# The first MLP product by Strassen's scheme on 576-token groups, its hidden rows passed through DRAM, in a hybrid diffusion layer on Trainium2

## The chip, the cores and the metric

The kernel runs on one core of one Trainium2 chip, in one launch. The metric is the device time of one execution in microseconds (us). TensorE multiplies matrices into PSUM (eight banks of 512 float32 columns per partition), VectorE, ScalarE and GpSimd do the elementwise work, and SyncE (SP) issues most of the DMAs. An engine carries out its instructions in the order in which they are written; engines wait for one another by semaphores.

## The reference, cut to what matters

One layer acts on 128 prompt tokens and 1024 sample tokens of width 1024. A mixer of retention and a diagonal state-space scan comes first, then its output projection with a residual and a row norm, then the MLP. The change concerns the MLP alone:

```python
h = _norm(x) * (1.0 + sc2) + sh2                       # (1152, 1024)
f = jnp.square(jax.nn.relu(h @ w_ff1 + b_ff1)) @ w_ff2 + b_ff2
x = _ln_affine(ALPHA * x + g2 * f, ln2_g, ln2_b)       # w_ff1 (1024, 4096), w_ff2 (4096, 1024)
```

The modulation `sc2, sh2, g2` of the prompt tokens differs from that of the sample tokens. Everything is float32.

## The kernel before, in words

A float32 operand x is split into a rounded part hi and a rest lo = x - hi, both of type float32r (`split`, L195: a copy on ScalarE or VectorE, a subtraction on VectorE or GpSimd). A product of two split operands is three matmuls, hi x hi, hi x lo and lo x hi, into one PSUM bank (`mm3`, L208 to L210). Most tiles of SBUF are 30 slots of 128 x 1152 words (`slot`, `rel`): a freed slot goes to the end of a list, and a new tile takes the head of it, so a tile waits for whoever used its slot before. The order of the instructions on each engine is the order in which this file writes them.

The 1152 tokens are nine row tiles ("slots" 0 to 8 in the code, `sl`) of 128. The output projection `op_mm` (L1472 to L1474) takes a row tile at a time, 48 matmuls of 512 columns; `op_a` and `op_b` make the residual, the row norm and its gain; `op_c` writes the row tile to DRAM (RD) and, for the row tiles 0 to 2, norms it again for the MLP. Between the projections of row tiles 5 and 6 `make_h2` transposes the normed row tiles, modulates them on ScalarE and splits them.

The MLP runs in three groups g of 384 tokens. Each group has 32 steps f, one for each 128 hidden units. In a step `ff1` makes 24 matmuls of 384 columns (8 blocks of the inner dimension, three each), ScalarE adds the bias, takes Relu and Square, and `split` makes the hidden rows for the second product. `ff2` adds this step's share to the six accumulators of the group: three row tiles, two halves, three matmuls of 512 columns each, 18 in all (L1620 to L1622). The loop writes `ff1` of step i+1 ahead of `ff2` of step i:

```python
        f_load(i + 3)
        f_split(i + 2, 0)
        f_split(i + 1, 1)
        ...
        if i + 1 < 3 * NF:
            ff1(i + 1)
        if g < 2 or f < NF - TAIL:
            ff2(i)
```

`f_load` has SP load a block of both weight matrices, 0.5 MB each (L1535, L1536); so each weight is loaded and split three times, once a group. `h2_prep` and `make_h2` make the next group's operand in steps 14 to 27 of a group. At a group's end `ep1` takes the accumulators out of PSUM times the gate (L1660), and `ep2` and `ep3` make the residual (L1665), the last row norm (L157 to L182), gain (L1668) and bias (L1669) and store the rows, in steps 1, 3 and 5 of the next group. In the last group the second product of the last six steps (TAIL) is kept to the end and done a row tile at a time, and `last_rows` ends the last tile.

Of the kernel before, what the change touches and what calls it, by code (L numbers as in the profile page):

```python
# [9 lines left out]
F32 = mybir.dt.float32  # L10
# [21 lines left out]
def kernel(  # L32
# [36 lines left out]
    free, held = list(range(NS)), {}  # L69

    def slot(name, dt=F32):

        i = free.pop(0)
        t = slots.tile([P, SLOTF], dt, tag=f"b{i}", name=nm(name), bufs=1)
        held[t.name] = i
        return t
# [1418 lines left out]
    def op_c(sl, x, *_):  # L1495
        a = x[:, 0:D]
        gl(RD[sl], a)
        if sl < 3:
# [6 lines left out]
    h2T = {}  # L1505

    def make_h2(g, k0=0, k1=KT):
        if k0 == 0:
            h2T[g] = group_slots("h2")
        at = h2T[g]  # L1510
        for kt in range(k0, k1):
            pt = ps("h2t")
            for i in range(3):
                PE.transpose(pt[:, i * P:(i + 1) * P], h2n[3 * g + i][:, kt * P:(kt + 1) * P], ident)
            h = t384("h")
            for a, b, cd in (((0, 128, 1), (128, 384, 0)) if g == 0 else ((0, 384, 0),)):
                S.activation(h[:, a:b], pt[:, a:b], AF.Identity, bias=modT[:, 24 + kt, cd:cd + 1], scale=modT[:, 32 + kt, cd:cd + 1])
            split(at(kt, 0), at(kt, 1), h, "v", "p")
        if k1 == KT:
            for i in range(3):  # L1520
                rel(h2n.pop(3 * g + i))
# [5 lines left out]
    fw = {}  # L1527

    def f_load(i):

        if i >= 3 * NF or i in fw:
            return
        f = i % NF
        r1, r2 = slot("w1r"), slot("w2r")
        ld(r1[:, 0:D].rearrange("p (k n) -> p k n", k=KT), w_ff1[0].rearrange("(k p) n -> p k n", p=P)[:, :, f * P:(f + 1) * P])  # L1535
        ld(r2[:, 0:D], w_ff2[0, f * P:(f + 1) * P, :])  # L1536
        fw[i] = [r1, r2]

    def f_split(i, which, leng="v"):
        if i >= 3 * NF:  # L1540
            return
        hi, lo = slot("wh", F32R), slot("wl", F32R)
        split(hi[:, 0:D], lo[:, 0:D], fw[i][which][:, 0:D], "s", leng)
        rel(fw[i][which])
        fw[i][which] = (hi, lo)

    pend = {}
    for sl in range(9):
# [15 lines left out]
        if sl == 5:  # L1564
            f_load(0)
        if sl == 6:
            f_split(0, 0, "v")
            f_split(0, 1, "p")
            f_load(1)
    for kt in range(4, 8):  # L1570
        rel(*wo[kt])
    f_load(2)
    if stop <= 6:
        for sl in range(9):
            t = slot("dbg")
            ld(t[:, 0:D], RD[sl])
            dump(f"x1_{sl}", t[:, 0:D])
        return


    fp = []

    def fvec(src):
        t = fp[0].tile([P, D], F32, tag="fvec", name=nm("fvec"), bufs=5)
        ld(t, src.partition_broadcast(P))
        return t

    hid, x1t = {}, {}

    def ff1(i):  # L1590
        g, f = divmod(i, NF)
        pu = ps("ff1")
        wh, wl = fw[i][0]
        for kt in range(KT):
            k = slice(kt * P, (kt + 1) * P)
            mm3(pu[:, 0:384], wh[:, k], wl[:, k], h2T[g](kt, 0), h2T[g](kt, 1), kt == 0, kt == KT - 1)
        r = t384("r")
        S.activation(r, pu[:, 0:384], AF.Relu, bias=bf1[:, f:f + 1])  # L1598
        S.activation(r, r, AF.Square)
        hh = slot("hid", F32R)[:, 0:768].rearrange("p (a n) -> p a n", a=2)  # L1600
# [3 lines left out]
        if f == NF - 1:  # L1604
            rel(*h2T[g].tiles.values())
# [186 lines left out]
```

## Time and profile before

| | |
|---|---|
| median of 3 runs (lowest to highest) | 1431.72 us (1427.59 to 1432.12) |
| the profiled execution, its time | 1430.16 us |
| its span in the trace | 1428.4 us |
| granted TensorE clock over the span, mean | 0.982 of 2.4 GHz |
| HBM read, written | 186.31 MB, 27.02 MB |

The page gives for each engine the time in which at least one of its instructions ran. TensorE's matmuls are pipelined: one lasts longer than the distance from its start to the next one's start, and it is that distance, called the pitch below, that adds up. A stage's table shows busy times in a stretch of the span; a timeline row shows the start and the duration of one instruction, or of several merged. Idle time in square brackets stands ahead of an instruction, with what ended it.

### The profile page before, as it was taken

The page shows a single profiled execution, that of the slowest core. Times are in us where ns is not written, and L with a number is a line of the kernel's source. Part 1 is how long each engine was busy: PE and PEld are TensorE (multiplying, and loading weights), DVE is VectorE, ACT ScalarE, POOL GpSimd, SP SyncE. Part 2 cuts the span into 40 slices and gives each one's busy share as a digit, 9 for nine tenths or more (in the row PEclk, how much of TensorE's full clock was granted, in tenths as well). Part 3 has the DMA queues.
Part 4 walks back from the last instruction along what each step waited for, and adds up shares of the span by engine and source line. Part 5 has one row for each costly group of instructions (what it writes and reads, how often), then busy time and mean ns, then how long its engine had stood idle before and what let it go on. Part 6 is the DMA issues. An engine that isn't in the chain of part 4 may idle for free.

```text
span 1428.4 us, 19630 instructions
## 1 busy us (share of the span) xinstructions
PE 1356.3 (95%) x7631; PEld 1223.9 (86%) x7631; DVE 817.9 (57%) x1477; ACT 593.7 (42%) x993; POOL 236.9 (17%) x298
## 2 busy tenths in 40 slices
PE   5899999996998899989999999999999999999996
PEld 2799799986987788879999999989999998999995
DVE  6597979693266767773444334654543367433346
ACT  4467112121435532344445543444544444444351
POOL 2600000563535212530000100100001001000002
PEclk9999999998999999999999999999999999999998
DMA  9435631756995151376353333474433424743321
GB/s 317 130 98 154 227 105 31 211 161 209 258 312 141 53 192 58 117 255 219 118 166 115 118 118 118 146 231 139 148 116 110 135 94 138 245 136 118 122 85 45
DMA packets 186813, 214.62 MB, mean 150 GB/s; under 512 B 20056, under 2 KB 150624, under 8 KB 186208
## 3 DMA queue, kind: packets, MB, share of 16 engines
q1 hardware_dynamic: 167968, 174.65, 38.5%
q0 software_dynamic: 9648, 31.52, 7.3%
q10 hardware_dynamic: 9104, 7.19, 1.6%
q8 instruction: 60, 0.98, 0.3%
q14 instruction: 33, 0.27, 0.1%
HBM read 186.31 MB, written 27.02 MB: 149 GB/s over the span
## 4 chain that ended last, share of the span: by engine, by line
PE 66%; DVE 14%; ACT 5%; issue 5%; DMA 4%; POOL 3%; SPq 0%; ACTq 0%; POOLq 0%; DVEq 0%
PE ff L210 8%; PE ff L208 8%; PE ff L209 8%; PE acc L1622 8%; PE acc L1621 8%; PE acc L1620 7%; PE pu L209 3%; PE pu L208 3%; PE pu L210 3%; DMA w1r<-in_w_ff_dram 2%; DMA SD<-SB 1%; PE pv L692 1%; DVE st L157 1%; DVE st L158 1%; DVE wl L201 1%
## 5 line engine op out<-in xcount | busy, mean ns | idle before, releaser
L201 DVE TENSOR_TENSOR hid<-r,hid 128x384 fp32r<-128x384 f32 x96 | 67.5, 703 | 339.6 <-ACT hid L200 339.4
L208 PE MATMUL ff<-h,wh 128*128 128x384 f32 x768 | 258.8, 337 | 0.0
L210 PE MATMUL ff<-h,wl 128*128 128x384 f32 x768 | 257.8, 336 | 0.1
L209 PE MATMUL ff<-h,wh 128*128 128x384 f32 x768 | 257.3, 335 | 0.0
L1622 PE MATMUL acc<-wh,hid 128*128 128x512 f32 x564 | 222.8, 395 | 5.0 <-DVE hid L201 5.0
L1620 PE MATMUL acc<-wh,hid 128*128 128x512 f32 x564 | 220.5, 391 | 4.3 <-ACT hid L200 4.3
L1621 PE MATMUL acc<-wl,hid 128*128 128x512 f32 x564 | 221.8, 393 | 0.0
L1598 ACT ACTIVATE r<-ff,bf 128x384 f32<-128x384 f32 x96 | 55.6, 579 | 304.8 <-PE ff L210 304.8
L208 PE MATMUL pu<-hTh,wh 128*128 128x384 f32 x480 | 165.6, 345 | 0.7 <-ACT hTh L571 0.7
L209 PE MATMUL pu<-hTl,wh 128*128 128x384 f32 x480 | 162.7, 339 | 1.5 <-DVE hTl L574 1.4
L210 PE MATMUL pu<-hTh,wl 128*128 128x384 f32 x480 | 161.7, 337 | 1.1 <-POOL wl L201 1.1
L201 DVE TENSOR_TENSOR wl<-w1r,wh 128x1024 fp32r<-128x1024 f32 x96 | 117.5, 1224 | 61.8 <-ACT wh L200 57.2
L208 PEld LDWEIGHTS ff<-h,wh 128*128 128x128 f32 x768 | 144.2, 188 | 2.9
L209 PEld LDWEIGHTS ff<-h,wh 128*128 128x128 f32 x768 | 144.2, 188 | 2.9
L210 PEld LDWEIGHTS ff<-h,wl 128*128 128x128 f32 x768 | 144.1, 188 | 0.5 <-DVE wl L201 0.5
L1622 PEld LDWEIGHTS acc<-wh,hid 128*128 128x128 f32 x564 | 106.4, 189 | 29.3 <-DVE hid L201 7.0
L1620 PEld LDWEIGHTS acc<-wh,hid 128*128 128x128 f32 x564 | 106.5, 189 | 24.8 <-ACT hid L200 4.9
L1621 PEld LDWEIGHTS acc<-wl,hid 128*128 128x128 f32 x564 | 106.4, 189 | 20.6
L201 DVE TENSOR_TENSOR wl<-w2r,wh 128x1024 fp32r<-128x1024 f32 x95 | 120.2, 1265 | 0.9 <-PE acc L1622 0.6
L200 ACT ACTIVATE wh<-w1r 128x1024 fp32r<-128x1024 f32 x96 | 100.5, 1047 | 28.4 <-DMA w1r<-in_w_ff_dram 27.9
L200 ACT ACTIVATE wh<-w2r 128x1024 fp32r<-128x1024 f32 x96 | 100.3, 1045 | 0.0
L208 PEld LDWEIGHTS pu<-hTh,wh 128*128 128x128 f32 x480 | 91.0, 190 | 6.7 <-issue 4.1
(480 smaller groups left out, 2089.4 us busy)
## 6 DMA issues: line engine op xcount, KB each, us to landing
w1r<-in_w_ff_dram SPq DMA_DIRECT2D x96, 512.0 KB, 4.5
w2r<-in_w_ff_dram SPq DMA_DIRECT2D x96, 512.0 KB, 5.1
wa<-in_w_ada_dram SPq DMA_DIRECT2D x48, 512.0 KB, 8.0
wr<-in_w_in_dram SPq DMA_DIRECT2D x20, 512.0 KB, 4.0
SD<-SB POOLq DMA_DIRECT2D x8, 576.0 KB, 12.5
WD<-W POOLq DMA_DIRECT2D x8, 576.0 KB, 4.1
RD<-xr POOLq DMA_DIRECT2D x9, 512.0 KB, 3.1
x<-RD SPq DMA_DIRECT2D x9, 512.0 KB, 7.6
```

The costliest lines, as they stand in the source:

```text
L157: V.bn_stats(st[:, 0], x[:, 0:512])
L158: V.bn_stats(st[:, 1], x[:, 512:1024])
L200: S.activation(hi, x, AF.Copy)
L201: (tt if leng == "v" else PO.tensor_tensor)(lo, x, hi.bitcast(F32), SUB)
L208: PE.matmul(out, lhsT=wh, rhs=xh, start=first, stop=False)
L209: PE.matmul(out, lhsT=wh, rhs=xl, start=False, stop=False)
L210: PE.matmul(out, lhsT=wl, rhs=xh, start=False, stop=last)
L692: PE.matmul(pv[64 * g2:64 * g2 + 64, l * NCOL:(l + 1) * NCOL], lhsT=W[:, g * P + ri * 64:g * P + ri * 64 + 64], rhs=X[:, g], start=True, s ...
L1598: S.activation(r, pu[:, 0:384], AF.Relu, bias=bf1[:, f:f + 1])
L1620: PE.matmul(o, lhsT=hh[:, 0, tk], rhs=wh[:, cs], start=(f == 0), stop=False)
L1621: PE.matmul(o, lhsT=hh[:, 0, tk], rhs=wl[:, cs], start=False, stop=False)
L1622: PE.matmul(o, lhsT=hh[:, 1, tk], rhs=wh[:, cs], start=False, stop=(f == NF - 1))
```

## The change

The first product is done for two groups of 576 tokens instead of three of 384. A group's operand h (1024 x 576) is cut into four blocks of 512 x 288, and a pair of weight blocks (1024 x 256) into four of 512 x 128. Strassen's scheme (in Winograd's form) makes the four result blocks of 128 x 288 from seven products of sums of blocks, each 4 x 3 = 12 matmuls of 288 columns. The sums of h are made once a group (`h2_sums`, two on VectorE and two on GpSimd, then `h2_split`). Those of the weights are made in each step (`f_prep`: two sums on VectorE, two on GpSimd, seven splits), one step ahead. The products are added up as they leave PSUM, by one copy on ScalarE and seven additions on VectorE.

The two products no longer take turns. The steps are: 16 of the first product for tokens 0 to 575, 32 of the second for tokens 0 to 383, 16 of the first for tokens 576 to 1151, then 32 and 32 of the second for the other two groups of 384 tokens. The hidden rows after the Square are written to a DRAM tensor HD by SP and loaded again, as float32, in the second product's steps, where they are split. The prompt and the next four row tiles are normed in the projection's loop now (`op_c`, five instead of three); twelve further slots replace the pool `fp`; the gates, gains and biases of the epilogue are loaded when they are needed and freed again; the first group's epilogue is moved into the second group's first product, with its additions and its gain on GpSimd.

```diff
+    HT = 288
+    def make_h2(g, kt):
+        if kt == 0:
+            BLK.update({(j, l): slot("hb") for j in range(2) for l in range(2)})
+        pa, pb = ps("h2t"), ps("h2t")
+        for i in range(4):
+            PE.transpose(pa[:, i * P:(i + 1) * P], h2n[i + 5 * g][:, kt * P:(kt + 1) * P], ident)
+        PE.transpose(pb[:, 0:P], h2n[4][:, kt * P:(kt + 1) * P], ident)
...
+        for o, x, cd in parts:
+            S.activation(o, x, AF.Identity, bias=modT[:, 24 + kt, cd:cd + 1], scale=modT[:, 32 + kt, cd:cd + 1])
...
+    def h2_sums(n):
+        b11, b12, b21, b22 = (BLK.get(k) for k in ((0, 0), (0, 1), (1, 0), (1, 1)))
+        if n == 0:
+            BLK["t1"] = slot("hb")
+            tt(BLK["t1"], b12, b11, SUB)
+        elif n == 1:
+            BLK["t2"] = slot("hb")
+            tt(BLK["t2"], b22, BLK["t1"], SUB)
+        elif n == 2:
+            PO.tensor_tensor(b12, b22, b12, SUB)
+        else:
+            BLK["t4"] = slot("hb")
+            PO.tensor_tensor(BLK["t4"], b21, BLK["t2"], SUB)
...
+    HD = drp.tile([NF, P, NTOK], F32, name="HD")
+    STEPS = [(1, 0, p) for p in range(16)] + [(2, 0, f) for f in range(NF)] + [(1, 1, p) for p in range(16)]
+    STEPS += [(2, g, f) for g in (1, 2) for f in range(NF)]
...
+    def f_prep(i):
+        if STEPS[i][0] == 2:
...
+            split(hi[:, 0:D], lo[:, 0:D], r[:, 0:D], "s")
...
+            split(hid[i][:, 0:384], hid[i][:, 384:768], h[:, 0:384], "s")
...
+        tt(s1, a21, a22, ADD)
+        tt(s2, s1, a11, SUB)
+        PO.tensor_tensor(s3, a11, a21, SUB)
+        PO.tensor_tensor(s4, a12, s2, SUB)
+        yield
+        for n, x in enumerate((a11, s2, s1, s3, a12, a22, s4)):
+            t = ops[n] = slot("wop", F32R)
+            split(t[:, 0:512], t[:, 512:D], x, "s")
...
+            yield
...
     for sl in range(9):
...
         if sl == 7:
-            f_split(1, 0, "v")
+            op_mm(7, 0, 4)
+            for kt in range(5, 8):
+                make_h2(0, kt)
+        x, po = op_mm(sl, 3 if sl < 3 else 4 if sl == 7 else 0)
+        if sl == 6:
+            for kt in range(5):
+                make_h2(0, kt)
+            f_load(0)
+        if sl == 7:
+            for n in range(4):
+                h2_sums(n)
+            h2_split(0)
...
+    op_c(7, *pend.pop(7))
+    prep(0, 2)
+    h2_split(1)
+    prep(0, 1)
...
+    h2_split(3, "p")
...
     def ff1(i):
...
+        for n in range(7):
+            o = bank[n] = ps("ff1")[:, 0:HT]
+            w, (xh, xl) = ops[n], hop[n]
+            for q in range(4):
+                wh, wl = w[:, q * P:(q + 1) * P], w[:, 512 + q * P:512 + (q + 1) * P]
+                xs = slice(q * HT, (q + 1) * HT)
+                mm3(o, wh, wl, xh[:, xs], xl[:, xs], q == 0, q == 3)
+            rel(w)
+            if n == 0:
+                S.copy(p1, o)
+            elif n == 1:
+                tt(u2, o, p1, ADD)
...
+            yield
...
+            S.activation(cv, cv, AF.Square)
+            ld(HD[2 * p + q][:, g * 576:(g + 1) * 576], cv)
...
+    for i, (kind, g, f) in enumerate(STEPS):
+        prep(i)
+        for j in range(i + 1, min(i + 4, NST)):
+            if STEPS[j][0] == 2 or j <= i + 2:
+                f_load(j)
+        if kind == 1:
...
+            if g == 1 and f in (2, 4, 6):
+                ep_add(f // 2 - 1, PO)
+            if g == 1 and f in (3, 5, 7):
+                ep2(f // 2 - 1, True)
...
+            prep(i + 1, 1)
+            for _ in ff1(i):
+                prep(i + 1, 1)
+            continue
+        if STEPS[i + 1][0] == 2 if i + 1 < NST else False:
+            prep(i + 1)
...
+        if g == 0:
+            if 1 <= f < 6:
+                h2_prep(9 - f)
+            if 8 <= f < 16:
+                make_h2(1, f - 8)
...
+        if g == 2 and f in (1, 3, 5):
+            sl = 3 + f // 2
+            ep_add(sl)
             ep2(sl)
             ep3(sl)
```

## Rows read from the trace of the kernel before

**Rows 1.** The page, part 1: engine, busy us (share of span), instructions.

```profile
PE 1356.3 (95%) x7631; PEld 1223.9 (86%) x7631; DVE 817.9 (57%) x1477; ACT 593.7 (42%) x993; POOL 236.9 (17%) x298
```

**Rows 2.** The page, part 4: the chain that ended last, by engine.

```profile
PE 66%; DVE 14%; ACT 5%; issue 5%; DMA 4%; POOL 3%; SPq 0%; ACTq 0%; POOLq 0%; DVEq 0%
```

**Rows 3.** Table of stages: stretch, us, busy by engine, granted clock, DMA, GB/s.

```profile
core 0: us, PE busy (x) PEld busy (x) DVE busy (x) ACT busy (x) POOL busy (x), PEclk, DMA share, GB/s
...
609.00:621.50 12.50, 7.10 (x21) 5.16 (x20) 10.10 (x21) 4.60 (x7) 2.90 (x2) 0.73 0.84 275
622.00:700.00 78.00, 77.86 (x396) 71.18 (x397) 38.05 (x35) 36.05 (x51) 9.49 (x4) 1.00 0.61 202
...
880.00:940.00 60.00, 57.54 (x290) 51.73 (x289) 42.34 (x59) 28.24 (x41) 7.16 (x3) 1.00 0.28 89
1150.00:1250.00 100.00, 98.63 (x497) 89.09 (x496) 61.21 (x77) 46.48 (x66) 7.19 (x3) 1.00 0.47 152
1250.00:1350.00 100.00, 100.00 (x508) 91.08 (x507) 36.18 (x37) 42.40 (x60) 0.00 (x0) 1.00 0.39 128
```

**Rows 4.** Timeline of TensorE, one MLP step: start us, duration us, instruction.

```profile
700.82 0.39 PE L1620 MATMUL acc<-wh,hid 128*128 128x512 f32 x1
...
704.94 0.33 PE L208 MATMUL ff<-h,wh 128*128 128x384 f32 x1
...
709.13 0.39 PE L1620 MATMUL acc<-wh,hid 128*128 128x512 f32 x1
```

**Rows 5.** Timeline of TensorE, matmuls and transposes of 128 columns (xN merged).

```profile
376.89 0.60 PE L1219 MATMUL pk<-ident,qkv 128*128 128x128 f32 x4
377.32 0.60 PE L1221 MATMUL pv<-ident,qkv 128*128 128x128 f32 x4
...
390.76 0.38 PE L1235 MATMUL pkf<-qkv,qkv 128*128 128x128 f32 x2
...
393.21 0.39 PE L1235 MATMUL pkb<-qkv,kb 128*128 128x128 f32 x2
```

**Rows 6.** Timeline of TensorE, start of the MLP.

```profile
608.91 0.34 PE L210 MATMUL ff<-h,wl 128*128 128x384 f32 x1
612.85 0.50 PE L1620 MATMUL acc<-wh,hid 128*128 128x512 f32 x1 [3.60 <-ACT hid L200]
...
621.49 0.34 PE L208 MATMUL ff<-h,wh 128*128 128x384 f32 x1
```

**Rows 7.** Timeline of VectorE, the last group's epilogue.

```profile
1401.50 1.23 DVE L1665 TENSOR_TENSOR o<-o,x 128x1024 f32<-128x1024 f32 x1
...
1407.17 1.22 DVE L1668 TENSOR_TENSOR o<-o,fvec 128x1024 f32<-128x1024 f32 x1 [1.37 <-ACT o L1667]
...
1409.66 2.35 DVE L1665 TENSOR_TENSOR o<-o,x 128x1024 f32<-128x1024 f32 x1
...
1417.83 1.57 DVE L1692 TENSOR_TENSOR o<-o,x 128x512 f32<-128x512 f32 x1
```

**Rows 8.** Timeline of GpSimd, the last group's epilogue.

```profile
1408.53 2.39 POOL L1669 TENSOR_TENSOR o<-o,fvec 128x1024 f32<-128x1024 f32 x1 [199.05 <-issue]
1416.49 2.35 POOL L1668 TENSOR_TENSOR o<-o,fvec 128x1024 f32<-128x1024 f32 x1 [5.57 <-ACT o L1667]
```

**Rows 9.** Timeline of VectorE, the subtractions of one MLP step.

```profile
702.75 0.56 DVE L201 TENSOR_TENSOR hid<-r,hid 128x384 fp32r<-128x384 f32 x1 [3.86 <-ACT hid L200]
...
703.70 1.23 DVE L201 TENSOR_TENSOR wl<-w1r,wh 128x1024 fp32r<-128x1024 f32 x1 [0.39 <-ACT wh L200]
704.84 1.22 DVE L201 TENSOR_TENSOR wl<-w2r,wh 128x1024 fp32r<-128x1024 f32 x1
```

**Rows 10.** The page, part 5: ScalarE's copy of a split: count, busy us, mean ns.

```profile
L200 ACT ACTIVATE wh<-w1r 128x1024 fp32r<-128x1024 f32 x96 | 100.5, 1047 | 28.4 <-DMA w1r<-in_w_ff_dram 27.9
```

**Rows 11.** The page, part 6: loads, KB each, median us from issue to landing.

```profile
w1r<-in_w_ff_dram SPq DMA_DIRECT2D x96, 512.0 KB, 4.5
```

More of the change, by code (lines that the diff above doesn't have):

```diff
@@ L67, in ps @@
         return psp.tile([P, 512], F32, tag="ps", name=nm(name))
-    free, held = list(range(NS)), {}
+    NX = 12
+    free, held, xpool = list(range(NS)), {}, []
     def slot(name, dt=F32):
         i = free.pop(0)
-        t = slots.tile([P, SLOTF], dt, tag=f"b{i}", name=nm(name), bufs=1)
+        t = (slots if i < NS else xpool[0]).tile([P, SLOTF], dt, tag=f"b{i}", name=nm(name), bufs=1)
         held[t.name] = i
@@ L1503, in op_c @@
             rel(x)
[L1505 to L1521, printed above, removed]
+    HT = 288
@@ L1524, with h2_split @@
+    def h2_split(n, leng="v"):
+        x = BLK.pop(HKEYS[n])
+        hop[n] = slot("hop", F32R), slot("hop", F32R)
+        split(*hop[n], x, "s", leng)
+        rel(x)
     NF = 32
@@ L1539, in f_split @@
-    def f_split(i, which, leng="v"):
-        if i >= 3 * NF:
-            return
[L1542 to L1545, printed above, removed]
+        kind, g, f = STEPS[i]
+        fw[i] = []
+        if kind == 1:
+            for q in range(2):
+                r = slot("w1r")
+                c0 = (2 * f + q) * P
+                ld(r[:, 0:D].rearrange("p (k n) -> p k n", k=KT), w_ff1[0].rearrange("(k p) n -> p k n", p=P)[:, :, c0:c0 + P])
+                fw[i].append(r)
+        else:
+            r = slot("w2r")
+            ld(r[:, 0:D], w_ff2[0, f * P:(f + 1) * P, :])
+            hid[i] = slot("hid")
+            ld(hid[i][:, 0:384], HD[f][:, g * 384:(g + 1) * 384])
+            fw[i].append(r)
@@ L1547, with prep @@
+    def prep(i, n=99):
+        if i >= NST:
+            return
+        if i not in preps:
+            f_load(i)
+            preps[i] = f_prep(i)
+        for _ in range(n):
+            if next(preps[i], 0) == 0:
+                break
     pend = {}
@@ L1563 @@
         op_b(sl, *pend[sl])
[L1564 to L1569, printed above, removed]
+    op_c(7, *pend.pop(7))
+    prep(0, 2)
+    h2_split(1)
+    prep(0, 1)
     for kt in range(4, 8):
         rel(*wo[kt])
[L1572 to L1581, printed above, removed]
+    h2_split(2)
@@ L1630, in x1_load @@
             sl = 3 * g + i
-            x1t[sl] = fp[0].tile([P, D], F32, tag="x1", name=nm("x1"), bufs=3)
-            ld(x1t[sl], RD[sl])
+            x1t[sl] = slot("x1")
+            ld(x1t[sl][:, 0:D], RD[sl])
     def h2_prep(sl):
@@ L1656, in ep1 @@
         gv = vecs["g2p" if sl == 0 else "g2s"]
-        o = fp[0].tile([P, D], F32, tag="o", name=nm("o"), bufs=3)
+        o = slot("o")
         for hf in range(2):
```

231 lines of the change are left out of this document (151 added, 80 removed).

## The prediction

> **What bounds the kernel now.** I read the page's busy shares first, then the chain that ended last, then a table of stages, then single steps of TensorE. The reader is to see TensorE busy for 1356 of 1428 us while VectorE stands at 57% and GpSimd at 17% [rows 1], and two thirds of the last chain on TensorE [rows 2]. In the table TensorE is never idle from 1250 to 1350 and for 77.86 of 78 us from 622 to 700, at the full granted clock (1.00, that is 2.4 GHz) [rows 3]. So in the MLP, from 600.7 us to the end, time is TensorE's instruction count times its pitch, plus a few stalls. One step there is 18 matmuls of the second product (700.82 to 704.94, 4.12 us, 0.2289 us each) and 24 of the first (704.94 to 709.13, 4.19 us, 0.1746 us each) [rows 4]. The stalls are at the start (last matmul of the opening at 608.91, next at 612.85, the first second-product step done only at 621.49, in a stage with granted clock 0.73 [rows 3, 6]) and at the two group changes (2.46 us idle in 880 to 940, 1.37 us in 1150 to 1250 [rows 3]).
>
> **The change part by part.** Rivals and range use the ends that I give.
>
> *First product.* Before: 96 steps of 24 matmuls, 2304 x 0.1746 = 402.3 us. After: 2 groups x 16 steps x 7 products x 12 matmuls = 2688 matmuls of 288 columns. No row has 288 columns. From 384 to 512 columns the pitch grows by (0.2289 - 0.1746)/128 = 0.000424 us a column, so the line gives 0.1339 us at 288. Ends: 288 columns at 2.4 GHz with nothing added, 0.1200; and the straight line between the 128-column matmuls (390.76 to 393.21, 22 of them, 0.1114 us [rows 5]) and 384, 0.1509. I take 0.1339, nearest to the 384 row: 2688 x 0.1339 = 359.9 us, a gain of 42.4 (ends: gain 79.7, loss 3.3).
>
> The Trainium skill (TensorE: Matmul & The Clock Gate, Back-to-back issue gap) gives columns/2.4 plus 2.5 ns, which would be 122.5 ns here, an estimate from that page, and another 31 us of gain. The rows do not bear it: 512 columns would be 216 ns and take 229, 384 would be 162.5 and take 175 [rows 4].
>
> *What feeds it.* Each 128x128 weight block pair now needs two sums on VectorE and two on GpSimd of 512 columns, and seven splits of 512 (a ScalarE copy and a VectorE subtraction each); each product is taken out of PSUM by VectorE operations of 288 columns, seven a step. VectorE: subtractions of 1024 start 1.14 us apart, and 1.23 against 0.56 us for 1024 against 384 columns is 1.04 ns a column [rows 9], so 512 columns cost 0.61, 288 cost 0.38, 1152 cost 1.27. A step: 9 x 0.61 + 7 x 0.38 + 0.2 for two dependent pairs = 8.4 us. ScalarE: 1.05 us for 1024 [rows 10] makes 0.55 for 512; seven of them, one copy of 288, and Relu and Square over 1152 in two halves each come to about 6.7 us. GpSimd: 2.39 us for 1024 [rows 8], 2.4 us for its two sums. TensorE's step is 84 x 0.1339 = 11.25 us. All three lie beside it. Operands for step i+1 are made product by product during step i, seven products ahead of their use, and eight PSUM banks hold a whole step, so VectorE may be some 8 us late before TensorE waits. One thing eats that reserve: a two-input VectorE operation on SBUF takes 2.35 us instead of 1.23 while GpSimd runs beside it (1409.66 against 1401.50; GpSimd 1408.53 to 1410.92) and the 512-column addition at 1417.83 takes 1.57 [rows 7, 8]. Per step that adds at most half of GpSimd's 2.4 us: 9.6 of 11.25. I cost it at nothing in plain steps.
>
> *Second product.* Its 1728 matmuls are unchanged, 4.12 us a step. In a step alone VectorE has 1.62 us (1024 and 384), ScalarE 1.5. The rows come from DRAM: 0.52 MB weights and 0.20 MB hidden rows in 4.12 us are 175 GB/s; 622 to 700 moved 202 GB/s at DMA share 0.61 with TensorE full [rows 3]. Loads are issued three steps ahead. Nothing.
>
> *Write and read of the hidden rows.* SP issues the write behind the Square, and behind it wait the weight loads of step i+2: they start about 3 us into a step, need about 5 (one 0.5 MB load lands in 4.5 [rows 11]) and are wanted at 11.25. Nothing, with 3 us of margin.
>
> *Opening.* Ahead of the last projection stand 40 transposes for 24: 16 x 0.109 us (376.89 to 377.32 is four [rows 5]) = 1.7, and about 1 us because each pair of banks waits for ScalarE's four evacuations. +2.7; later 40 for 48, -0.9. Sum +1.8 (ends 0.5 and 5).
>
> *Start of the first product.* After the last slot but one VectorE has two block sums and one block split (3.8 us), the slot's residual and norm (4 x 0.61 + 3.07 = 5.5, the norm worked out below from rows 7), its gain (1.2 after ScalarE), then nine operations of 512 and three of 1152 (9.3); GpSimd has two block sums, an addition, two weight sums and three block splits, some 18 us. TensorE covers 11.0 us of this with the last projection (48 x 0.2289) and then drains products at 1.6 us each. Uncontended, the last block split is ready about 2 us late; with both engines at the contended rate of rows 7, about 13 us late. I take 10.4, nearer to the contended end since GpSimd is busy throughout. Before, 609.08 to 621.49 held 4.12 us of work: 8.3 lost [rows 6]. Net +2 (ends -6 and +8; a granted clock of 0.73 again would lie in the upper part).
>
> *Second product of the first group.* In steps 1 to 4 VectorE has 1.62 plus a row norm of 3.07 (1401.50 + 1.23 to 1407.17 - 1.37 [rows 7]), 4.7 against 4.12, and the first norm waits for a row load queued behind the last hidden write. +3 (0 to 6).
>
> *Epilogues.* Those of tokens 0 to 383 move into the second group's first product, on GpSimd (2.4 + 4.8 us per row tile over six steps): VectorE's step there reaches about 13 us against 11.25 for six steps, 10 us, of which the reserve takes 8. +2 (0 to 8). Those of tokens 384 to 767 fall into second-product steps of 4.12 us. VectorE has six preparations and three chains (1401.50 to 1408.31, 6.8 us, mostly in-order waits on ScalarE) and 1.2 us contention each: 6 x 1.62 + 3 x 6.8 + 3 x 1.2 = 33.7, from 2.4 us after the group's end, against 7 x 4.12 = 28.8: TensorE waits 7.3. Before, the same chains lay in steps of 8.3 us. +7.3 (2 to 13). The group-change losses of before (3.8) go: -3.8 (0 to -3.8). The tail of six steps is unchanged.
>
> Sum: -42.4 + 1.8 + 2 + 3 + 2 + 7.3 - 3.8 = -30.1. The profiled execution took 1430.16 us (span 1428.4), so 1400.1; the median of the runs is 1.6 higher, so I say 1400.
>
> **Rivals.**
> - *The feed is hidden better.* VectorE runs ahead across group changes and the two stall terms vanish: -42.4 + 1.8 - 3.8 + 2 = -42, 1388; with a start 6 us better 1380. For it: idle VectorE before those steps. Against: the row norms are in order on VectorE.
> - *Each narrow matmul pays more.* If loading 128 weight columns cannot hide behind 288, the pitch goes to the upper end, 0.1509: +45.7 on the sum, 1446, slower than before. It decides for slower from 0.1451 us on (30.1/2688 more than I take). For it: 128-column matmuls go no faster than 0.1114 us. Against: that is still below 0.12.
> - *VectorE becomes the bound of the first product.* Place: all 32 steps. It takes over beyond 11.25 us a step and undoes the whole gain at 12.2. If all nine two-input operations ran at the contended rate the step would be 13.9 us and the kernel 32 x 2.65 = 85 us longer, 1485; half of that, 1440. For it: rows 7 and 8. Against: GpSimd works 2.4 us of the 11.25. The Trainium skill (VectorE: DVE Perf Modes, Two Vector instructions with no wait between them) says that the second SBUF input of such an operation is read through an interface shared with GpSimd; that would make it general for all nine splits and sums, where the rows show three operations.
> - *SP's queue holds the weights back.* If loads behind the hidden write land 5 us later than rows 11 say, each first-product step is 2 us longer: +64, 1464.
> - *The narrow matmuls carry nothing extra.* At 0.1200 us the first product is 37 us shorter, 1363. Against: both widths of rows 4 carry 14 to 16 ns beyond their columns.
>
> **How the numbers follow.** About 0.3% (4.3 us) is what these runs can tell from no change. Forecast (1385 to 1416) 0.58; feed hidden better 0.15; no extra per matmul 0.03; pitch higher 0.10; VectorE bound 0.10; SP queue 0.04. The pitch and VectorE cases are spread from a little above the forecast to far above, so of their 0.24 some 0.07 is still faster and 0.05 the same. Faster 0.83, same 0.05, slower 0.12. Range 1378 to 1430: below, better feed; above, half of the pitch and VectorE cases.
>
> **What would show it.** Right: first-product matmuls of 288 columns at about 0.134 us start to start, steps of 11.2 to 11.4 us, TensorE's table full in both first-product stages, VectorE at 75 to 90% there, 4.12 us a step in the second product, waits on VectorE of 7 us in all in the first steps of the third group, and about 10 us lost at the start. Wrong: a pitch above 0.14, TensorE waiting for weight operands in plain steps, second-product steps above 4.3 us, or waits for DMA on the hidden rows.

## The result and the profile after

The changed kernel takes 1494.15 us (median of 4 runs, 1490.91 to 1496.3) against 1431.92 us for the kernel before on the same chip (4 runs, 1427.59 to 1436.95): ratio 1.0431, 95% interval 1.0391 to 1.0472. It is slower by 62 us; the forecast was 1400. Its profiled execution took 1495.43 us, span 1493.6, against 1430.16 before.

The page of the changed kernel: part 1, part 4 and two DMA groups of part 6, which answer to [rows 1, 2, 11].

```profile
PE 1362.9 (91%) x8023; PEld 1205.7 (81%) x8023; DVE 1026.4 (69%) x1879; ACT 630.4 (42%) x1128; POOL 359.8 (24%) x351
...
PE 14%; DVE 3%; DMA 1%; ACT 1%; issue 0%; POOL 0%; SPq 0%; POOLq 0%; DVEq 0%; ACTq 0%
...
w1r<-in_w_ff_dram SPq DMA_DIRECT2D x64, 512.0 KB, 5.5
...
hid<-HD SPq DMA_DIRECT2D x96, 192.0 KB, 4.5
```

TensorE's busy time is nearly that of before, its share fell from 95% to 91%, and no other engine is near full. The chain can be followed back only through the last fifth of the span here, so the stages have to tell. The next table has the columns of [rows 3]; its rows are the end of the opening, the first product's start (three and a half of its four long steps), the rest of that stage, the second product of the first group, the second first-product stage in two halves, and the second product of the other two groups in two parts.

```profile
560.00:614.30 54.30, 45.74 (x210) 37.82 (x209) 37.44 (x78) 24.51 (x49) 20.21 (x10) 0.91 0.23 78
614.30:684.00 69.70, 47.32 (x275) 43.99 (x274) 55.58 (x69) 27.55 (x44) 30.17 (x16) 0.82 0.33 93
684.00:837.30 153.30, 151.05 (x1071) 144.36 (x1070) 115.58 (x200) 86.06 (x153) 35.31 (x23) 0.99 0.47 134
837.80:991.00 153.20, 144.67 (x616) 115.19 (x617) 99.11 (x133) 74.74 (x113) 20.36 (x7) 0.97 0.61 206
991.10:1100.00 108.90, 98.38 (x673) 93.80 (x671) 85.23 (x136) 50.16 (x88) 39.49 (x20) 0.95 0.38 111
1100.00:1204.00 104.00, 97.60 (x673) 92.08 (x672) 78.99 (x135) 56.79 (x101) 30.24 (x18) 0.97 0.47 137
1204.40:1260.00 55.60, 52.97 (x215) 42.39 (x216) 35.72 (x46) 27.47 (x38) 2.41 (x1) 0.94 0.84 312
1260.00:1480.00 220.00, 213.06 (x928) 174.82 (x927) 117.32 (x156) 73.09 (x101) 12.16 (x4) 0.99 0.46 162
```

The two first-product stages take 223.0 us (614.3 to 837.3) and 212.8 (991.1 to 1203.9), where 16 steps at TensorE's own speed are 179.2; the forecast had about 190 and 182. From the start of the first matmul of each step (84 a step), the lengths of the 16 steps of either stage are:

```
first group    29.0 15.5 16.2 18.0 | 11.2 11.6 11.9 11.9 ... 12.3 to 12.9 now and then
second group   11.2 11.2 11.2 13.0 17.4 15.5 17.4 15.5 16.3 | 11.9 11.9 ...
```

**A plain step.** TensorE, in one of the steps of 11.9 us. Columns as in [rows 4].

```profile
739.79 0.29 PE L209 MATMUL ff<-hop,wop 128*128 128x288 f32 x1
739.92 0.29 PE L210 MATMUL ff<-hop,wop 128*128 128x288 f32 x1
740.32 0.40 PE L211 MATMUL ff<-hop,wop 128*128 128x288 f32 x1
...
742.03 0.40 PE L211 MATMUL ff<-hop,wop 128*128 128x288 f32 x1
```

The matmuls start 0.133 us apart (the median over the kernel too), which is the forecast's 0.1339. But the one at 740.32 comes 0.40 after its forerunner. VectorE in the same step shows what it waited for:

```profile
739.58 0.69 DVE L202 TENSOR_TENSOR wop<-w1r,wop 128x512 fp32r<-128x512 f32 x1
...
740.55 1.42 DVE L202 TENSOR_TENSOR wop<-ws,wop 128x512 fp32r<-128x512 f32 x1
...
745.28 0.45 DVE L1707 TENSOR_TENSOR hc<-ff,hc 128x288 f32<-128x288 f32 x1
747.09 0.69 DVE L202 TENSOR_TENSOR wop<-w1r,wop 128x512 fp32r<-128x512 f32 x1 [1.36 <-ACT wop L201]
...
749.52 0.69 DVE L202 TENSOR_TENSOR wop<-ws,wop 128x512 fp32r<-128x512 f32 x1 [1.37 <-ACT wop L201]
...
751.49 0.69 DVE L202 TENSOR_TENSOR wop<-w1r,wop 128x512 fp32r<-128x512 f32 x1
```

The matmul at 740.32 (L211) is the third of a product that began at 739.79, and the first that reads the rest lo of the product's weights; the subtraction that ends at 740.27 makes that lo. The one that ends at 741.97 makes it for the next product, whose third matmul starts at 742.03. So operands meant to be seven products ahead arrive just in time: VectorE is a whole step late. From 739.58 to 751.49 its step is 11.91 us, and in it stand two idle times of 1.36 and 1.37 us, both ended by ScalarE. ScalarE's list at that place:

```profile
745.76 0.78 ACT L1708 ACTIVATE hc<-hc,bf 128x576 f32<-128x576 f32 x1 [3.90 <-DVE hc L1707]
746.45 0.61 ACT L201 ACTIVATE wop<-w1r 128x512 fp32r<-128x512 f32 x1
748.19 0.78 ACT L1711 ACTIVATE hc<-hc,bf 128x576 f32<-128x576 f32 x1 [1.13 <-DVE hc L1710]
748.87 0.62 ACT L201 ACTIVATE wop<-ws 128x512 fp32r<-128x512 f32 x1
```

Behind VectorE's addition (L1707, ends 745.73) ScalarE does a Relu, and only behind that the weight copy that VectorE's next subtraction needs; the addition, Relu, copy and subtraction follow one another, twice a step. ScalarE itself idled 3.90 us ahead of the Relu. VectorE is busy for only 75% of this stage (115.58 of 153.30), and yet its list is longer than TensorE's step: 8.4 us of work, 0.74 of standstill (the 1.42 at 740.55, whose kind takes 0.68 alone) and 2.73 of waiting make 11.9. That TensorE's row says 151.05 of 153.30 busy hides it: a matmul is drawn 0.29 long or more but they start 0.133 apart, so a start that comes up to 0.16 late leaves no idle time. The length of the step shows it.

**The start.** The last wait of TensorE in the opening (waited for: us, times, longest):

```profile
PE h2t L1518 <- ACT xr L1501: 8.5, 1, 8.5
```

The first product begins at 614.3, where the MLP of before began at 600.7. Then VectorE and GpSimd from there:

```profile
617.82 3.46 DVE L202 TENSOR_TENSOR wop<-w1r,wop 128x512 fp32r<-128x512 f32 x1
...
625.53 3.82 DVE L202 TENSOR_TENSOR hop<-hb,hop 128x1152 fp32r<-128x1152 f32 x1
...
639.83 0.69 DVE L1604 TENSOR_TENSOR ws<-w1r 128x512 f32<-128x512 f32 x1 [3.79 <-DMA w1r<-in_w_ff_dram]
```

```profile
618.22 1.28 POOL L1606 TENSOR_TENSOR ws<-w1r,w1r 128x512 f32<-128x512 f32 x1
619.46 1.26 POOL L1607 TENSOR_TENSOR ws<-w1r,ws 128x512 f32<-128x512 f32 x1
621.32 10.50 POOL L202 TENSOR_TENSOR hop<-hb,hop 128x1152 fp32r<-128x1152 f32 x3 [0.61 <-ACT hop L201]
```

A subtraction of 512 columns that takes 0.69 alone takes 3.46, and ends 0.56 after GpSimd's two sums (620.72). The two engines take turns; neither goes on at half speed. At 639.83 VectorE also waits 3.79 us for the load of the next step's weights.

Part of the loss is the clock. In the four steps its granted share is 0.83 on the mean: behind several of its waits TensorE is at 1.2 GHz for some us, as from 632.83 to 638.11, where 22 matmuls start 0.24 us apart. 64 such matmuls cost about 7 of the 34 us that the four steps lose; the waits cost the rest.

**The second product.** Its matmuls start 0.227 us apart (0.2289 in [rows 4]). But the first seven steps of the first group take 7.5, 6.6, 6.7, 6.9, 6.9, 6.9 and 5.1 us for 4.1, the first two of the second group 7.5 and 7.5, and five of the third group's first steps 6.2, 4.7, 9.0, 4.1, 6.4. TensorE's waits from 837.8 to 991, and VectorE in that stretch:

```profile
PE acc L1739 <- ACT hid L201: 7.1, 4, 2.6
```

```profile
852.79 0.69 DVE L158 BATCH_NORM_STATS2 st<-h2n 128x6 f32<-128x512 f32 x1 [4.65 <-DMA h2n<-RD]
...
858.08 1.23 DVE L202 TENSOR_TENSOR wl<-w2r,wh 128x1024 fp32r<-128x1024 f32 x1 [2.25 <-ACT wh L201]
```

**The epilogue in the second first-product stage.** Waits of ScalarE from 1024 to 1110, and of TensorE from 1020 on:

```profile
ACT wop L201 <- POOL ws L1606: 15.2, 3, 5.1
```

```profile
PE ff L209 <- ACT wop L201: 8.5, 3, 3.5
PE ff L211 <- DVE wop L202: 6.2, 9, 1.6
```

GpSimd's weight sums stand in its list behind the epilogue's operations of 1024 columns, ScalarE's copies wait for the sums, and TensorE for the copies. But the steps stay as long without that order, as e2 and c2 below show.

### The profile page after: what moved, and what is told of

Same layout as the page of the kernel before. It is cut to its first block, busy times and chain, and to the rows that moved or that the text cites. A ratio compares the mean times of both kernels' runs of the same rounds, so it can differ in the third digit from the quotient of the medians.

```text
span 1493.6 us, 21468 instructions
## 1 busy us (share of the span) xinstructions
PE 1362.9 (91%) x8023; PEld 1205.7 (81%) x8023; DVE 1026.4 (69%) x1879; ACT 630.4 (42%) x1128; POOL 359.8 (24%) x351
## 5 line engine op out<-in xcount | busy, mean ns | idle before, releaser
L211 PE MATMUL ff<-hop,wop 128*128 128x288 f32 x896 | 278.5, 311 | 24.0 <-DVE wop L202 21.8
L209 PE MATMUL ff<-hop,wop 128*128 128x288 f32 x896 | 272.7, 304 | 15.4 <-ACT wop L201 12.7
L210 PE MATMUL ff<-hop,wop 128*128 128x288 f32 x896 | 270.3, 302 | 2.0 <-DVE hop L202 2.0
L1739 PE MATMUL acc<-wh,hid 128*128 128x512 f32 x564 | 225.1, 399 | 10.7 <-ACT hid L201 10.5
L1741 PE MATMUL acc<-wh,hid 128*128 128x512 f32 x564 | 224.7, 398 | 6.0 <-DVE hid L202 6.0
L211 PEld LDWEIGHTS ff<-hop,wop 128*128 128x128 f32 x896 | 174.1, 194 | 39.0 <-DVE wop L202 37.5
L209 PEld LDWEIGHTS ff<-hop,wop 128*128 128x128 f32 x896 | 174.3, 194 | 19.9 <-ACT wop L201 17.8
L210 PEld LDWEIGHTS ff<-hop,wop 128*128 128x128 f32 x896 | 174.3, 195 | 2.3 <-DVE hop L202 2.3
L211 PE MATMUL pu<-hTh,wl 128*128 128x384 f32 x480 | 162.3, 338 | 1.1 <-POOL wl L202 1.1
L202 DVE TENSOR_TENSOR wop<-ws,wop 128x512 fp32r<-128x512 f32 x128 | 124.2, 972 | 43.5 <-ACT wop L201 43.4
L1739 PEld LDWEIGHTS acc<-wh,hid 128*128 128x128 f32 x564 | 108.2, 192 | 35.8 <-ACT hid L201 14.1
L1741 PEld LDWEIGHTS acc<-wh,hid 128*128 128x128 f32 x564 | 108.1, 192 | 31.9 <-DVE hid L202 9.3
L202 DVE TENSOR_TENSOR wop<-w1r,wop 128x512 fp32r<-128x512 f32 x96 | 81.2, 848 | 43.9 <-ACT wop L201 43.9
L210 PEld LDWEIGHTS pu<-hTl,wh 128*128 128x128 f32 x480 | 91.4, 190 | 4.1 <-DVE hTl L575 4.0
L211 PEld LDWEIGHTS pu<-hTh,wl 128*128 128x128 f32 x480 | 91.4, 190 | 1.7 <-POOL wl L202 1.7
## 6 DMA issues: line engine op xcount, KB each, us to landing
SD<-SB POOLq DMA_DIRECT2D x8, 576.0 KB, 12.5
```

The source lines that it names most:

```text
L202: (tt if leng == "v" else PO.tensor_tensor)(lo, x, hi.bitcast(F32), SUB)
L209: PE.matmul(out, lhsT=wh, rhs=xh, start=first, stop=False)
L210: PE.matmul(out, lhsT=wh, rhs=xl, start=False, stop=False)
L211: PE.matmul(out, lhsT=wl, rhs=xh, start=False, stop=last)
L1739: PE.matmul(o, lhsT=hh[:, 0, tk], rhs=wh[:, cs], start=(f == 0), stop=False)
L1741: PE.matmul(o, lhsT=hh[:, 1, tk], rhs=wh[:, cs], start=False, stop=(f == NF - 1))
```

## The experiments

Each ratio is to the kernel before, run on the same chip, with its 95% interval; the changed kernel stands at 1.0431. e1 to e4 ran on one chip, c1 to c4 on another, c5 and c6 on a third, so a difference in us between two of them is good to a few us. Step lengths are read as above.

**e1_relu_late: Relu behind the weight copies.** Both Relus of a step move behind its last weight copy on ScalarE.

```diff
                 tt(c21, o, c21, ADD)
-                S.activation(C[:, 2 * HT:], C[:, 2 * HT:], AF.Relu, bias=bf1[:, 2 * p + 1:2 * p + 2])
...
                 tt(c12, o, c12, ADD)
-                S.activation(C[:, 0:2 * HT], C[:, 0:2 * HT], AF.Relu, bias=bf1[:, 2 * p:2 * p + 1])
...
             cv = C[:, q * 576:(q + 1) * 576]
+            S.activation(cv, cv, AF.Relu, bias=bf1[:, 2 * p + q:2 * p + q + 1])
             S.activation(cv, cv, AF.Square)
```

> Of the changed kernel (1494 us) only ScalarE's order differs: both Relus of a first-product step stand behind the last two weight copies instead of ahead of them. Theory A (VectorE waits twice a step, 1.36 us each, in order on ScalarE's Relu, so its step is 11.9 us, and the step of backlog from the start is never worked off): VectorE's step falls to about 10.2 us, plain steps of the first product go from 11.9 to 11.2 us once the backlog is gone, and the stages behind them start with less backlog: 1455 to 1478 us. Theory B (plain steps are long because VectorE's two-input operations stand still while GpSimd makes its two weight sums): no more than 5 us off, 1489 to 1495, plain steps still 11.9.

1446.5 us, 1.0121 (1.0079 to 1.0163): two instructions in another place give back 48 of the 62 us, more than expected. Every plain step takes 11.2; the steps at the start 29.3, 13.0, 13.4, 16.8; those with the epilogue 12.4, 15.9, 12.5, 14.7, 11.6; and the first two steps of both second-product stages 4.1 and 4.6 where they took 6.6 to 7.5, since VectorE no longer enters them late. Of the 48 us the plain steps are 15.6; the rest is saved in the later steps of the start, in the steps with the epilogue and in the first steps of the second product. The stage's row, and VectorE in a plain step:

```profile
688.60:823.00 134.40, 134.40 (x1010) 134.40 (x1010) 117.94 (x196) 82.00 (x144) 30.02 (x22) 1.00 0.53 155
```

```profile
733.43 0.45 DVE L1707 TENSOR_TENSOR hc<-ff,hc 128x288 f32<-128x288 f32 x1
733.79 0.68 DVE L202 TENSOR_TENSOR wop<-w1r,wop 128x512 fp32r<-128x512 f32 x1
```

The subtraction follows the addition with no idle time between; VectorE is now 88% busy (117.94 of 134.40) and TensorE never waits.

**e2_sums_vector: the weight sums on VectorE alone.**

```diff
-        PO.tensor_tensor(s3, a11, a21, SUB)
-        PO.tensor_tensor(s4, a12, s2, SUB)
+        tt(s3, a11, a21, SUB)
+        tt(s4, a12, s2, SUB)
```

> Of the changed kernel only the two weight sums of each step move from GpSimd to VectorE. Theory B: VectorE loses 1.8 us of standing still a step and gains 1.2 us of work; plain steps go to 11.3 us or less, and the six long steps of the second group (13 to 17.4 us), where GpSimd's sums queue behind the epilogue, lose half of their excess: 1465 to 1480 us. Theory A: VectorE's step is 8.4 + 1.2 of work + 2.7 of waits = 12.3 us, so plain steps get longer, to 12.0 to 12.4 us; the time stays within 1485 to 1505 us, the second group's long steps excepted.

1493.44 us, 1.045 (1.0419 to 1.048): no gain. Plain steps take 12.3 to 12.4, the first one of the stage 23.8 for 29.0. VectorE behind the two waits of a step:

```profile
755.31 0.69 DVE L202 TENSOR_TENSOR wop<-w1r,wop 128x512 fp32r<-128x512 f32 x1 [1.37 <-ACT wop L201]
...
757.74 0.69 DVE L202 TENSOR_TENSOR wop<-ws,wop 128x512 fp32r<-128x512 f32 x1 [1.37 <-ACT wop L201]
```

GpSimd does nothing in these steps and the two waits stay. The step is 8.4 + 1.2 (two sums more) + 2.74 = 12.3. So in plain steps GpSimd's standstill is the small part (0.74 a step) and ScalarE's order the large one.

The five steps with the epilogue take 17.8, 15.8, 18.2, 15.5 and 18.4 us, 29.7 beyond 11.2 a step, where the changed kernel has 27.9 in six. GpSimd's list has no weight sums here, so the loss doesn't need their place behind the epilogue.

**e3_epilogue_later: the first group's epilogue moved** from the second group's first product to steps 8 to 24 of its second product, by the code that the other groups use, its additions and its gain on VectorE.

```diff
-            if g == 1 and f in (2, 4, 6):
-                ep_add(f // 2 - 1, PO)
-            if g == 1 and f in (3, 5, 7):
-                ep2(f // 2 - 1, True)
...
+        if g == 1 and f in (8, 14, 20):
+            ep_add((f - 8) // 6)
+            ep2((f - 8) // 6)
+        if g == 1 and f in (12, 18, 24):
+            ep3((f - 12) // 6)
```

> Of the changed kernel only the first group's epilogue moves, out of the second group's first product into steps 8 to 24 of the second group's second product, its addition and gain on VectorE. Theory C (the epilogue's GpSimd work and row norms cost the second first-product stage 27 us): that stage falls from 212.8 to 180 to 190 us with steps of 11.2 us throughout, the second group's second product grows by 0 to 4 us, total 1462 to 1475 us. Rival (those steps are long because of weight loads or the backlog of VectorE): stage stays above 200 us, total above 1483 us.

1469.58 us, 1.0283 (1.0253 to 1.0313). The second first-product stage takes 185.8 us for 212.8: nine steps of 11.2 and then 12.3, 11.9, 12.1, 12.8, 11.9. The steps with the epilogue are gone, and the nine show the reserve at work: with VectorE 0.7 us a step slower than TensorE, a lead of some 6 us lasts nine steps, and then each step costs what VectorE needs.

**e4_transposes_later: four pairs of the opening's transposes from ahead of row tile 7's last matmuls to behind them.**

```diff
             op_mm(7, 0, 4)
-            for kt in range(5, 8):
+            for kt in range(4):
                 make_h2(0, kt)
...
         if sl == 6:
-            for kt in range(5):
-                make_h2(0, kt)
             f_load(0)
         if sl == 7:
+            for kt in range(4, 8):
+                make_h2(0, kt)
```

> Of the changed kernel only the place of the 40 opening transposes moves: four blocks in the middle of the projection of row tile 7, four after it, instead of five after tile 6 and three in the middle of tile 7. Theory D (TensorE stands 8.5 us for the second norm of row tile 4, which is late because two row norms lie on VectorE in one slot): the 8.5 us wait goes, the first product starts 8 to 10 us earlier, total 1482 to 1489 us. Rival (the start is bound by VectorE's list in front of the first product, so what is saved ahead is waited for there): the first product's first step grows by as much, total 1491 to 1497 us.

1504.51 us, 1.0527 (1.0497 to 1.0558): 10 us slower still, and above both ranges. TensorE waits less for the norm (3.0 for 8.5), but 5.1 us for ScalarE's evacuations and 2.9 for VectorE, and the first product starts at 622.6; its first step stays at 29.4. VectorE's waits from 560 to 640 have

```profile
DVE hb L1540 <- ACT hb L1527: 8.9, 1, 8.9
```

The block sums now wait for ScalarE's later evacuations, and all that is behind them in VectorE's list is later. So this edit only shifts the waits and doesn't tell what the 8.5 us are worth; c3 does.

**c1_relu_epilogue: e1 and e3 together.**

> Both earlier edits together: Relus behind the weight copies, and the first group's epilogue in the second group's second product. Theory A and C (two separate causes, which also feed each other through the backlog): second first-product stage 180 to 182 us, all its steps 11.2 us, total 1428 to 1436 us. If both edits gained by the same route, the sum is smaller: 1438 to 1446 us.

1435.25 us (8 runs), 1.002 (1.0006 to 1.0033). The second first-product stage takes 179.4 us, all its steps 11.2. The epilogue's cost on top of e1 was 11 us (25 in e3 alone). The two gains, 48 and 25, overlap by 14; that both delays draw on VectorE's one reserve is my reading of it.

**c2_relu_startvector: e1, and GpSimd's share of the first product on VectorE** (block sums, splits of the blocks, weight sums); the second weight pair is loaded earlier.

```diff
-            PO.tensor_tensor(b12, b22, b12, SUB)
+            tt(b12, b22, b12, SUB)
...
-    h2_split(3, "p")
+    h2_split(3)
...
+    f_load(1)
     h2_split(2)
```

> On top of the Relu edit (1446 us) everything that GpSimd does for the first product (two block sums, three block splits, two weight sums a step) goes to VectorE, and the weight loads of step 1 are issued ahead of the last block splits. Theory E (a two-input VectorE operation on SBUF stands still until the GpSimd operation beside it ends, so GpSimd's 10.5 us of block splits give VectorE nothing and cost it the same time): the first four steps fall from 72.5 to 55 to 62 us, VectorE's 512-column splits there from 3.1 to 3.5 us to 0.69, total 1428 to 1437 us. Rival (half rate: GpSimd does take work off VectorE, and VectorE's list is what binds the start): 7 us more work on VectorE, first four steps 75 to 80 us, total 1448 to 1455 us.

1437.22 us, 1.0046 (1.0026 to 1.0067), 9 less than e1, just above the ranges of theory E and far below the rival's. The first four steps take 20.3, 11.6, 15.3, 15.8, in sum 63.0 for e1's 72.5. From its first weight sum to its last split for the first step VectorE takes 16.5 us (613.37 to 629.84) for e1's 21.6 (616.28 to 637.88). It does more and is done 5 us sooner, since nothing stands still there:

```profile
617.93 0.68 DVE L202 TENSOR_TENSOR wop<-w1r,wop 128x512 fp32r<-128x512 f32 x1
618.53 1.34 DVE L202 TENSOR_TENSOR hop<-hb,hop 128x1152 fp32r<-128x1152 f32 x1
```

The other 4 us of the first step are VectorE's wait for the next weights' load (4.0 in e1), which is gone here. The epilogue is still on GpSimd in the second group's first product, and its steps lose 12.9 us beyond 11.2 each (11.2 in e1), though no weight sum is left in GpSimd's list. VectorE and GpSimd there, for one row tile:

```profile
1027.38 2.88 DVE L1607 TENSOR_TENSOR ws<-w1r,ws 128x512 f32<-128x512 f32 x1
1030.19 2.83 DVE L202 TENSOR_TENSOR wop<-w1r,wop 128x512 fp32r<-128x512 f32 x1
...
1033.31 2.50 DVE L202 TENSOR_TENSOR wop<-ws,wop 128x512 fp32r<-128x512 f32 x1
```

```profile
1026.96 2.76 POOL L1794 TENSOR_TENSOR o<-o,fvec 128x1024 f32<-128x1024 f32 x1 [19.68 <-ACT o L1793]
1029.80 2.67 POOL L1795 TENSOR_TENSOR o<-o,fvec 128x1024 f32<-128x1024 f32 x1
1032.43 2.82 POOL L1787 TENSOR_TENSOR o<-o,x 128x1024 f32<-128x1024 f32 x1
```

Each of the three VectorE operations ends 0.54 to 0.56 us after the GpSimd operation beside it: 6.1 us of standing still per row tile, on top of the row norm.

**c3_relu_actorder: e1, and a row tile's first norm on ScalarE ahead of the previous tile's second norm.**

```diff
         pend[sl] = op_a(sl, x, po)
+        op_n(sl, *pend[sl])
         if sl >= 1:
```

> On top of the Relu edit the norm of a row tile on ScalarE stands ahead of the second norm of the row tile before it, so VectorE's row norm lies where it waited. Theory D (with five tiles normed twice, VectorE's list of a row tile is longer than TensorE's 10.9 us, 2.5 us of it waits on ScalarE; TensorE then stands 8.5 us for row tile 4): the 8.5 us wait falls below 2 us and the first product starts 7 to 9 us earlier; total 1437 to 1440 us if what lies behind keeps its length, 1444 to 1447 us if the first step grows by as much, as it did when the transposes were moved.

1436.99 us, 1.0023 (0.9997 to 1.0049). The wait of 8.5 us is gone, the first product starts at 605.9 for 616.1 in e1, and its first step takes 29.5 as before: 9.5 us less, so what lies behind keeps its length.

**c5_norms_spread and c6_two_ahead: the second product, on c1.** In the first the five row norms stand in every second step and the second group's epilogue in steps 2 to 13 (the transposes, sums and splits behind the norms follow three steps later); in the second the operands are made two steps ahead.

```diff
-            if 1 <= f < 6:
-                h2_prep(9 - f)
+            if f in (1, 3, 5, 7, 9):
+                h2_prep(8 - f // 2)
...
-        if g == 2 and f in (1, 3, 5):
+        if g == 2 and f in (2, 6, 10):
```

```diff
             prep(i + 1)
+            if lead and i + 2 < NST and STEPS[i + 2][0] == 2:
+                prep(i + 2)
```

> c1_relu_epilogue (1435.25 us) with two further moves and no more: the five row norms for the next group's operand stand in every second step of the second product instead of in five steps in a row, and the second group's epilogue is spread over steps 2 to 13 of the third group. Left in c1 are 13.6 us beyond 4.1 us a step in steps 1 to 7 of the first second-product stage and 9.9 us in the first steps of the third group. Theory F (latency: the operands of a step are made only one step ahead, so each norm ahead of them in VectorE's and ScalarE's lists costs its 2.8 us of TensorE wherever it stands): nearly nothing is saved, the steps with a norm still take 6.5 to 7 us and those between 4.1, 1428 to 1436. Rival G (VectorE's work over the stretch is what counts, and the slack of the steps between pays for it): both excesses go, 1411 to 1417.

> c1_relu_epilogue (1435.25 us) with one further move and no more: second-product operands are made two steps ahead in the first twelve steps of a group and in the whole of the last one (their loads are issued four steps ahead); the norms stay in five steps in a row. Theory F (latency): the second step of lead (4.1 us) absorbs the first norm or two of the row of five and most of the three of the epilogue, which stand in every second step: 10 us of the 23.5 gone, 1420 to 1428. Rival G (VectorE's work over the stretch counts): five norms in a row stay as late as before beyond the first 4 us, and the third group's start loses as before: 1431 to 1436.

c5: 1419.94 us, 0.9914 (0.9889 to 0.9939). The third group's first steps lose nothing; in the first group 8.3 and 7.2 are left in steps 2 and 3, and from step 4 on it is 4.1, but for the steps with transposes (4.7). c6: 1431.11 us, 0.9991 (0.9973 to 1.0009): 4.1, 5.9, 6.9, 6.9, 6.9, 5.6 from step 2 to 7, and 4.4, 7.4, 4.7, 8.9 in the third group. By the lengths of its second-product stages c6 is 2.4 us shorter than c1. In c5 TensorE's one wait in the first group's second product, and the wait of VectorE ahead of it:

```profile
PE acc L1738 <- ACT hid L201: 4.1, 1, 4.1
```

```profile
833.50 0.70 DVE L158 BATCH_NORM_STATS2 st<-h2n 128x6 f32<-128x512 f32 x1 [4.87 <-DMA h2n<-RD]
```

c5 came out 8 us below the range of theory F and 3 above G's: G holds for the third group and for three of the five norms. c6 gave 4 us, at the edge of G. So for all norms but the first it is VectorE's load over the stretch that counts, and one step more of lead only swallows the first delay. Steps 2 and 3 stay long in c5 because of the first norm, by the trace: VectorE waits 4.87 us for its row, whose load SP issues behind the last hidden write, and the hidden rows of the next step stand behind that norm in ScalarE's list. Moving that load was not tried; with both moves, in c4, the two steps take 4.1 and 5.3.

**c4_all: all of these moves together.**

> All edits together, and in the second product the row norms of the next group's operand every second step, the second group's epilogue every fourth step, and operands made two steps ahead. If the stalls found add up: first product 2 x 180 us plus 12 us at the start, second product 395 us plus 6 us of transposes and some 5 us of waits, start of the first product at 606 us: 1395 to 1410 us, faster than the kernel before by 1.5 to 2.4%. If VectorE's list simply moves the waits on: 1415 to 1430 us.

1393.82 us (4 runs, 1391.41 to 1396.71), 0.9734 (0.971 to 0.9758): 39 us below the kernel before on that chip, 1 below the first of the expected ranges, and 100 below the change as made. The parts add up to 1397: c1's 1435.25, less 9.3 (c2 against e1), 9.5 (c3 against e1), 15.3 (c5) and 4.1 (c6); by the ratios they give 0.971. Its stages:

```profile
602.70:666.10 63.40, 51.45 (x337) 49.87 (x338) 58.77 (x96) 35.87 (x58) 6.46 (x4) 0.89 0.36 107
666.10:800.60 134.50, 134.50 (x1011) 134.50 (x1010) 114.78 (x215) 81.03 (x142) 0.00 (x0) 1.00 0.52 152
800.60:939.90 139.30, 137.84 (x619) 111.88 (x618) 91.24 (x129) 73.98 (x112) 12.57 (x2) 1.00 0.63 219
939.90:1119.10 179.20, 179.20 (x1346) 179.20 (x1345) 150.98 (x280) 106.05 (x185) 0.00 (x0) 1.00 0.47 139
1119.10:1380.00 260.90, 260.90 (x1151) 215.75 (x1150) 173.78 (x232) 103.32 (x145) 24.91 (x8) 1.00 0.57 206
```

TensorE is never idle from 666 to 800 and from 940 to 1380. What is left is the start: 63.4 us for four steps of 11.2, with VectorE busy for 58.77 of them.

## Why the prediction was wrong

By its own terms (us; the losses are a stage's length less its steps at 11.2 or 4.09, and less 4.4 for the 40 transposes in the second product):

| term | forecast | measured | from |
|---|---|---|---|
| first product's matmuls | -42.4 | -44.8 | 2688 x 0.133 against 402.3 |
| second product's matmuls | 0 | -2.9 | 96 x (4.09 - 4.12) |
| opening | +1.8 | +12.7 | 614.3 - 600.7, less 0.9 for 8 transposes fewer later |
| start of the first product | +2 | +25.6 | 78.7 - 4 x 11.2 = 33.9, less 8.3 |
| plain steps | 0 | +15.6 | 9.9 and 5.7 in the two stages |
| second product, first group | +3 | +18 | 153.3 - 130.9 - 4.4 |
| epilogue in the first product | +2 | +27.9 | 13.0 + 82.1 - 6 x 11.2 |
| second product, second group, first two steps | 0 | +6.4 | 15.0 against 8.6 in c4 |
| epilogue in the third group | +7.3 | +10 | 30.4 for five steps of 4.08 |
| losses at group changes | -3.8 | -3.8 | none are left |
| sum | -30.1 | +64.7 | profiled 1495.43 - 1430.16 = +65.3 |

**The step that failed** is "What feeds it", at "All three lie beside it ... I cost it at nothing in plain steps". The work in it was right: VectorE's 8.4 us a step is what e2 shows (12.3 less 1.2 less 2.74), and VectorE's share, 75%, is in the range that I gave. What I left out is that VectorE and ScalarE hand each other operands in order, so that a step lasts work plus waits. In the last epilogue I counted such waits ("mostly in-order waits on ScalarE", from the 1.37 us of [rows 7]); in the first product I didn't look in the diff where Relu stands. e1 shows it: the same work in another order, 48 us less, and plain steps at TensorE's 11.2. That is half of the 95 us between forecast and result, 15.6 of it in plain steps; the other half lies in the terms told below. The rival "VectorE becomes the bound of the first product", at 0.10, named the place. That its price, 1485, comes near the result is luck: it counts 2.65 us in each of 32 steps, where plain steps lose 0.7. Its reason (contended operations) gives 0.74 of the 3.5 us that a plain step has beyond VectorE's work, and e2 sets it aside there; beside the first step's block splits and beside the epilogue it holds (c2).

**The reserve** exists (some 6 us by e3, where I had 8), but not when it is wanted. At the start VectorE is already late, and with a step of 11.9 against 11.2 it can't catch up. In the second stage the reserve is there and lasts nine steps (e3). I took it as standing; it is spent once.

**The start** failed twice. The opening's 8.5 us came from ScalarE's order (c3), for which I had no term at all; with that wait gone the first product starts 10 us earlier. And I took contention as a slower rate ("at the contended rate"). The rows that I had read fit a standstill better: 2.35 us at 1409.66 ends 1.1 us after GpSimd's operation does (1410.92 [rows 7, 8]), about the 1.23 that it takes alone. The Trainium skill (SBUF — State Buffer, Who interferes with whom) says so: a VectorE instruction with two SBUF inputs contends with a GpSimd instruction that reads SBUF, and the port pair that they share is an exclusive lock. The runs agree that one engine stands still, with 3.46 us for 0.69, and in c2, which leaves GpSimd out, VectorE's list for the first step is 5 us shorter than in e1 though VectorE does more. The load of the next weights, 4 us of waiting that I had not counted, and the lower clock behind TensorE's waits add to the start's +25.6.

**The epilogue among first-product steps** was argued from VectorE's load (13 us against 11.25, eight of ten from the reserve). The waits named the order in GpSimd's list, 15.2 us in which ScalarE waits for weight sums behind the epilogue; but with those sums on VectorE the steps are no shorter (e2, c2). What I priced too low is that VectorE stands still while GpSimd does the epilogue's operations: 6.1 us a row tile in c2, where the three operations on VectorE itself would take 3.7, an estimate from 1.23 each [rows 7]. c1 shows 11 us for this stage once Relu is out of the way; the rest of the +27.9 went with the Relus (e1).

**The second product's early steps**: I had the load right (4.7 us of VectorE against 4.12) and not the waits: a norm takes turns with ScalarE, and steps with one took 6.7 to 6.9. About 4 of the +18 are the first two steps, which VectorE enters late, as it does the second group's (+6.4): in e1, without that lateness, 14 are left. The third group's epilogue (+10 for +7.3) came out inside its range. c5 takes the 10 away whole and 5 of the 13 that c1 has in the first group; in c4 4 are left there.

**What was right**: the pitch of 0.1339 (0.133), against both rivals on it; the second product at 4.1 us a step; the hidden rows through DRAM at nothing: no plain second-product step waits for them (4.1 us throughout c4's last stage from its third step on), and SP's queue did no harm to plain first-product steps (11.2 in e1). The formula of the Trainium skill that the prediction set aside (TensorE: Matmul & The Clock Gate, Back-to-back issue gap) is given there for an isolated matmul, so the rows of a stream don't speak against it. Hidden feeding in plain steps alone would not have made the forecast hold: e1 has it and takes 1446.5. It took the moves of c4 at the start, in the norms and in the epilogues as well to come to 1393.8.

## What to carry to other kernels

When a change gives an engine more work beside TensorE, write out the lists of all engines of one step in order and take the length of the longest loop through them, waits included; an engine at 75% can be the bound, and a lead only helps where the feeder's step is shorter than the consumer's. Look first at what stands ahead of a copy that another engine waits for: moving two Relus was worth 48 us. Work on GpSimd beside VectorE operations with two inputs in SBUF is not free: in this kernel its time was largely VectorE's too.

## What the hardware showed that I had not expected

- VectorE's operation at 617.82 is recorded as begun 0.4 us ahead of the first of two GpSimd sums, and still it ends behind both of them. GpSimd seems to stand still in its turn: its three splits of 1152 columns took 3.5 us each (10.50 / 3), where 1024 columns took 2.39 [rows 8].
- A VectorE operation with one operand in PSUM is not held: the product of 512 columns with the gate at 606.33 in the changed kernel took 0.69 us amid a GpSimd operation that ran from 605.15 to 608.96.
- The extra time of a matmul over its columns at 2.4 GHz is nearly the same at 288 columns (133 - 120 = 13 ns) and at 512 (227 - 213 = 14), each matmul with a weight load; the straight line through 384 and 512 columns held down to 288.
